# Later start and closer spacing of the modulation sums in a conditioned decoder layer

## The chip, the cores and the metric

The kernel runs on one core of one Trainium2 chip. The metric is the device time of one execution in microseconds (us); lower is better. A core has TensorE (PE, with its weight loads shown as PEld), VectorE (DVE), ScalarE (ACT), GpSimd (POOL) and SyncE (SP), each with its own queue of instructions that it takes in order. Here SP issues all transfers that are named below.

## The reference

One decoder layer on x (1024 tokens by 1024 columns, float32), conditioned by a vector c. Its matrix products are made to float32 accuracy. What matters for the change:

```
mod = silu(c) @ ada_w + ada_b            # 9 blocks of 1024: sh1 sc1 g1 sh2 sc2 g2 sh3 sc3 g3
h = rms_norm(x, norm_g[0]) * (1 + sc1) + sh1
x = x + 0.5 * g1 * ((silu(h @ w1) * (h @ w3)) @ w2)        # first feed-forward
...                                       # mixer with sh2 sc2 g2, second feed-forward with sh3 sc3 g3
```

Blocks 0 and 1 (sh1, sc1) are needed at once. Block 2 (g1) is needed when the first feed-forward's down products are added to x, blocks 3 and 4 for the norm behind that, and blocks 5 to 7 later.

## The kernel before, in words

The program is written in stages: the first feed-forward's up products (units), its down products (rounds), the mixer, and the second feed-forward in the same form. Within a stage the order of instructions is set by a planner (class Plan, L133). Each operation is given to it with an engine, an assumed duration, the tiles it reads and writes, and a rank, which is the time at which it is due. The planner goes through an assumed timeline, takes for each engine the operation that can start first, and among those that can start within 0.2 us the one of lowest rank. So the ranks and the assumed durations fix the order in which each engine gets its work, SP's queue too; the chip then runs each queue in that order.

**The up stage.** The hidden columns are treated in 11 parts of 256 (p = 0 to 10). A fast form of block multiplication with seven products instead of eight is used, numbered i = 1 to 7. A unit (p, i, m) is one product for one of the two weights m; there are 154 units. The first 12 are products 1 and 2 of the first three parts, units 12 to 41 are the other five products of these parts, ten units each, and from unit 42 on a part has fourteen units. A unit's matrix work (Ffn.products, L468) is four groups of three matmuls (mm3, L63, lines 64 to 66), because each operand is split into a rounded high part and a rest. The weights of a unit are split by ScalarE (cast, L57) and VectorE (rest, L60). Some units need sums of weight blocks first (minus, L391 to L395, on VectorE). After a unit its bank is read out by ScalarE (L505, L514) or added by VectorE (L496, L516, L520), and gate and value are multiplied (L524). The hidden blocks and their differences (hidden, L531) go to DRAM. Seven weight buffers (wh and wf) let the weights run ahead of TensorE.

Unit n is due at due1(n) (L906), 2.58 us apart from unit 12 on, and when(n) (L379) is the high part of unit n's weights: an operation with after=when(n) can't start before that cast.

**The modulation's blocks for later parts** are summed on VectorE beside these units (ada_half, L948). Blocks 2 to 7 are cut into halves of 512 columns, so there are twelve halves. For each, eight transfers bring 128 by 512 rows of ada_w (256 KB each, into three buffers named ar), and VectorE multiplies the first by a column of silu(c) (L943) and adds the next seven (L945) in one accumulator (acc, one buffer for all halves). The sum is split in two (ahl, L57 and L60), two matmuls with a matrix of ones add it over the partitions into a bank (psb, L968 and L969), and VectorE turns that row into columns of modc with four multiply-and-sum operations by the identity (ada_columns, L974, line 978) and one to three small ones (L982 to L987). The loop over the halves is at L989 to L993:

```
    halves = [(b, hf) for b in range(2, 8) for hf in range(2)]
    for n, (b, hf) in enumerate(halves):
        u = 24 + 9 * n
        ada_half(f1, b, hf, due1(u), 2.8, f1.when(u - 2), lambda ps, b=b, hf=hf: ada_columns(b, hf, ps), 1.3,
                 w=[("mod", b, hf)])
```

The loads of a half wait for the weights of unit u - 2. Its sums are due from due1(u) on, 2.8 us apart, and its two matmuls 22.4 us after due1(u), 8.7 units later.

**Behind the last half** come eight bias tables for the attention (bias_table, L996). The first waits for the last half, ("mod", 7, 1), and each next one for the store of the one before. Each has one float32 matmul into a bank named psw (L1003) that lies where psb did (tags tr and av). Then come the lambda and gate columns (lam_and_rnn_columns, L1054), a chain of small VectorE operations with two exponentials on ScalarE. The first round of the down stage (Ffn.down, L616) uses the banks tr and av.

Of the kernel before, what the change touches and what calls it, by code (L numbers as in the profile page):

```python
# [44 lines left out]
def layer(tc, I, out):  # L45
# [860 lines left out]
    def due1(n, k=0):  # L906
        if n < 4 * EARLY:
            return 21.0 + 5.0 * (4 * (n // 6) + k) + T_MM3 * (n % 6)
        return 62.0 + 2.58 * (n - 4 * EARLY)
# [38 lines left out]
    def ada_half(f, b, hf, at, pace, when, finish, dur, r=(), w=()):  # L948
        plan = f.plan
        op, the = plan.op, plan.get  # L950
        acc, ps = f"acc{b}_{hf}", f"psb{b}_{hf}"
        new_tile(plan, acc, "acc")
        for k in range(KC):
            a = f"ar{b}_{hf}_{k}"
            new_tile(plan, a, "ar")
            op(SP, lambda a=a, k=k: load(the(a), ada_v[:, k, b * D + hf * TG : b * D + (hf + 1) * TG]), T_LOAD,
               w=[a], rank=at + pace * k - 6, after=when)
            op(DVE, lambda a=a, k=k: ada_sum(the(acc), the(a), k), 0.66, r=[a] + ([acc] if k else []),
               w=[acc, (acc, k)], rank=at + pace * k)
        hl = [f"ahl{b}_{hf}_{s}" for s in range(2)]  # L960
        for s in hl:
            new_tile(plan, s, "k2", None, F32R)
        at += pace * KC
        f.split(lambda: the(hl[0]), lambda: the(hl[1]), lambda: the(acc), [acc], at, hl, hl[1:])
        new_tile(plan, ps, ("tr", "av"))

        def sums():
            T.matmul(the(ps), lhsT=onesr, rhs=the(hl[1]), start=True, stop=False)  # L968
            T.matmul(the(ps), lhsT=onesr, rhs=the(hl[0]), start=False, stop=True)  # L969

        op(PE, sums, 0.43, r=hl, w=[ps], rank=at)
        op(DVE, lambda: finish(the(ps)), dur, r=[ps, *r], w=w, rank=at)

    def ada_columns(b, hf, ps):  # L974
        c0 = b * KC + hf * 4
        for q in range(4):
            junk = fp.tile([P, P], F32, tag="arow", bufs=1, name=f"junk{b}_{hf}_{q}")
            V.tensor_tensor_reduce(
                junk, ps[:, q * P : (q + 1) * P], ident, 1.0, 0.0, ALU.mult, ALU.add, modc[:, c0 + q : c0 + q + 1]
            )  # L980
        mc = modc[:, c0 : c0 + 4]
        V.tensor_tensor(mc, mc, adabc[:, c0 : c0 + 4], ALU.add)  # L982
        if b % 3 == 1:
            o = b // 3 * KC + hf * 4
            V.scalar_tensor_tensor(gmc[:, o : o + 4], mc, 1.0, smc[:, NG0 + o : NG0 + o + 4], ALU.add, ALU.mult)
        if b == 2:
            V.tensor_scalar(mc, mc, 0.5, None, ALU.mult)  # L987

    halves = [(b, hf) for b in range(2, 8) for hf in range(2)]  # L989
    for n, (b, hf) in enumerate(halves):  # L990
        u = 24 + 9 * n
        ada_half(f1, b, hf, due1(u), 2.8, f1.when(u - 2), lambda ps, b=b, hf=hf: ada_columns(b, hf, ps), 1.3,
                 w=[("mod", b, hf)])  # L993

# [744 lines left out]
    for j in range(2):  # L1739
        n = next(nch)  # L1740
# [43 lines left out]
    for dc in range(KC):  # L1784
        n = n0 + dc
# [11 lines left out]
    for dc in range(6):  # L1797
        n = n0 + 8 + dc
# [104 lines left out]
    for hf in range(2):  # L1903
        u, row = 60 + 30 * hf, f"g3r{hf}"
# [132 lines left out]
def build(shapes):  # L2037
    import concourse.bacc as _bacc
    import concourse.tile as _tile

    nc = _bacc.Bacc("TRN2", target_bir_lowering=False, num_devices=1)
    aps = {n: nc.dram_tensor(f"in_{n}", s, F32, kind="ExternalInput").ap() for n, s in shapes.items()}
    out = nc.dram_tensor("out_0", (1, S, D), F32, kind="ExternalOutput").ap()
    with _tile.TileContext(nc, schedule_with_timeline_sim=True) as tc:
        layer(tc, aps, out)
    return nc
# [10 lines left out]
```

## Time and profile before

| | us |
|---|---|
| Runs of the kernel before | 1819.23, 1821.06, 1826.95 |
| Median of the three | 1821.06 |
| The profiled execution's own time | 1820.87 |
| Its span | 1818.3 |
| Mean granted TensorE clock in it | 0.989 of full speed |

The profile is of one execution. Times in it are counted from the span's start. The page gives busy time per engine and 40 slices of the span; the trace answers closer questions, by stretch, by instruction, by wait. "x" before a number is a count. L-numbers are lines of the kernel. Matmuls are pipelined, so the recorded duration of one is longer than the step from one start to the next. In lists in order of time the bracket at the end tells how long the engine was idle before the instruction and what ended that.

### The profile page before, as it was taken

To read this page: it belongs to the slowest core of one execution; us is meant where nothing else is said; L and a number is where in the kernel's file an instruction comes from. 1 tells how busy PE (TensorE), PEld (TensorE's weight loads), DVE (VectorE), ACT (ScalarE), POOL (GpSimd) and SP (SyncE) were. 2 spreads that over 40 slices of the span, in tenths; PEclk is the share of its full clock that TensorE was granted. 3 is DMA by queue.
4 is the path that set the end of the run, shared out by engine and by line. 5 is a ranking of instruction groups with operands and counts; after the bars stand their busy time and mean duration, and the time that the engine had idled before them with its cause. 6 is when DMAs were issued, how large, how long until landed. Compare 5 with 4: busy or idle time off the path is not lost.

```text
span 1818.3 us, 23531 instructions
## 1 busy us (share of the span) xinstructions
PE 1772.9 (98%) x8098; PEld 1456.2 (80%) x8098; DVE 1432.1 (79%) x2739; ACT 854.3 (47%) x1485; POOL 13.0 (1%) x28
## 2 busy tenths in 40 slices
PE   8999999999999999899999989999999999999997
PEld 7877788887788888688888878878888888888886
DVE  3898999887778779788787786598777666579798
ACT  4442443333554334676675854353333333365344
POOL 0000000000000001000000000000000000000000
PEclk8999999999999999999999989999999999999999
DMA  9636666553598663212121435315433333497862
GB/s 272 210 128 229 194 203 207 173 194 118 193 350 272 223 237 121 65 47 76 47 64 58 122 99 180 118 56 174 162 116 128 132 106 109 132 364 266 291 216 93
DMA packets 230136, 297.48 MB, mean 164 GB/s; under 512 B 16733, under 2 KB 125438, under 8 KB 230018
## 3 DMA queue, kind: packets, MB, share of 16 engines
q1 hardware_dynamic: 230018, 296.00, 49.5%
q8 instruction: 63, 1.03, 0.2%
q14 instruction: 55, 0.45, 0.1%
HBM read 228.30 MB, written 63.44 MB: 160 GB/s over the span
## 4 chain that ended last, share of the span: by engine, by line
PE 84%; DVE 9%; DMA 3%; ACT 2%; issue 1%; SPq 1%; DVEq 0%; ACTq 0%
PE f1b L64 6%; PE f2b L64 6%; PE f2b L66 6%; PE f2b L65 6%; PE f1b L66 6%; PE f1b L65 6%; PE pc L64 5%; PE pc L65 5%; PE pc L66 5%; PE f1ps L64 4%; PE f1ps L66 4%; PE f1ps L65 4%; PE f2ps L64 4%; PE f2ps L65 4%; PE f2ps L66 4%; PE psd L879 2%
## 5 line engine op out<-in xcount | busy, mean ns | idle before, releaser
L65 PE MATMUL f1b<-f1B,f1w 128*128 128x512 f32 x616 | 243.0, 394 | 5.7 <-DVE f1w L60 5.6
L64 PE MATMUL f1b<-f1B,f1w 128*128 128x512 f32 x616 | 245.3, 398 | 0.8 <-ACT f1vs L514 0.8
L66 PE MATMUL f1b<-f1B,f1w 128*128 128x512 f32 x616 | 242.4, 394 | 0.0
L64 PE MATMUL f2b<-f2B,f2w 128*128 128x512 f32 x440 | 171.5, 390 | 2.4 <-ACT f2vq L490 1.8
L65 PE MATMUL f2b<-f2B,f2w 128*128 128x512 f32 x440 | 171.5, 390 | 1.2 <-DVE f2w L60 1.2
L66 PE MATMUL f2b<-f2B,f2w 128*128 128x512 f32 x440 | 171.2, 389 | 0.0
L65 PEld LDWEIGHTS f1b<-f1B,f1w 128*128 128x128 f32 x616 | 116.3, 189 | 33.3 <-DVE f1w L60 8.8
L64 PEld LDWEIGHTS f1b<-f1B,f1w 128*128 128x128 f32 x616 | 116.3, 189 | 28.7 <-issue 2.7
L66 PEld LDWEIGHTS f1b<-f1B,f1w 128*128 128x128 f32 x616 | 116.2, 189 | 26.0
L60 DVE TENSOR_TENSOR f2w<-f2r,f2w 128x512 fp32r<-128x512 f32 x124 | 84.5, 688 | 66.2 <-ACT f2w L57 65.2
L64 PE MATMUL pc<-h,wch 128*128 128x512 f32 x320 | 131.1, 410 | 3.1 <-DVE h L1132 1.4
L57 ACT ACTIVATE f2w<-f2r 128x512 fp32r<-128x512 f32 x124 | 76.5, 628 | 110.8 <-issue 42.7
L66 PE MATMUL pc<-h,wch 128*128 128x512 f32 x320 | 125.7, 393 | 0.0
L65 PE MATMUL pc<-h,wcl 128*128 128x512 f32 x320 | 125.6, 393 | 0.0
L64 PE MATMUL f1ps<-f1o,f1d 128*128 128x512 f32 x308 | 121.6, 395 | 0.0
L57 ACT ACTIVATE f1w<-f1r 128x512 fp32r<-128x512 f32 x124 | 75.7, 627 | 97.0 <-DVE f1r L393 31.3
L66 PE MATMUL f1ps<-f1o,f1d 128*128 128x512 f32 x308 | 121.2, 393 | 0.0
L65 PE MATMUL f1ps<-f1o,f1d 128*128 128x512 f32 x308 | 121.0, 393 | 0.0
L64 PE MATMUL f2ps<-f2d,f2o 128*128 128x512 f32 x308 | 119.9, 389 | 0.1
L65 PE MATMUL f2ps<-f2d,f2o 128*128 128x512 f32 x308 | 119.8, 389 | 0.0
L66 PE MATMUL f2ps<-f2d,f2o 128*128 128x512 f32 x308 | 119.8, 389 | 0.0
L64 PEld LDWEIGHTS f2b<-f2B,f2w 128*128 128x128 f32 x440 | 82.6, 188 | 20.6 <-ACT f2vq L490 2.2
(414 smaller groups left out, 3944.3 us busy)
## 6 DMA issues: line engine op xcount, KB each, us to landing
ar<-in_ada_w SPq DMA_DIRECT2D x112, 256.0 KB, 3.3
f2r<-in_ffn_w SPq DMA_DIRECT2D x44, 512.0 KB, 3.7
f1r<-in_ffn_w SPq DMA_DIRECT2D x40, 512.0 KB, 4.0
f1wa<-in_ffn_w SPq DMA_DIRECT2D x38, 512.0 KB, 4.8
f2wa<-in_ffn_w SPq DMA_DIRECT2D x38, 512.0 KB, 5.6
f1b<-f1gt SPq DMA_DIRECT2D x44, 256.0 KB, 4.8
f2b<-f2gt SPq DMA_DIRECT2D x44, 256.0 KB, 5.7
rc<-in_w_in SPq DMA_DIRECT2D x20, 512.0 KB, 3.8
```

The lines of the kernel that those rows point to most:

```text
L57: A.activation(hi, src, AF.Copy)
L60: (eng or V).tensor_tensor(lo, src, hi.bitcast(F32), ALU.subtract)
L64: T.matmul(ps, lhsT=wh, rhs=xl, start=first, stop=False, skip_group_check=more)
L65: T.matmul(ps, lhsT=wl, rhs=xh, start=False, stop=False, skip_group_check=more)
L66: T.matmul(ps, lhsT=wh, rhs=xh, start=False, stop=last, skip_group_check=more)
L879: T.matmul(the(ps)[:, b : b + 1], lhsT=the(aw)[:, n, :], rhs=cact[:, 4 * h + n : 4 * h + n + 1], start=h == 0 and n == 0, stop=h == 1 and ...
```

## The change

The first half is put at unit 40 in place of unit 24, and the distance from one half to the next is eight units in place of nine. So the halves stand at units 40, 48, ... 128, where they stood at 24, 33, ... 123. The pace within a half, 2.8 us from one row to the next, stays as it is. The bias tables and the columns behind them keep their own due times (due1(128) on, and due1(142)).

```
     halves = [(b, hf) for b in range(2, 8) for hf in range(2)]
     for n, (b, hf) in enumerate(halves):
-        u = 24 + 9 * n
+        u = 40 + 8 * n
         ada_half(f1, b, hf, due1(u), 2.8, f1.when(u - 2), lambda ps, b=b, hf=hf: ada_columns(b, hf, ps), 1.3,
                  w=[("mod", b, hf)])
```

## Rows read from the trace of the kernel before

**Rows 1.** The page: busy time per engine, and VectorE's slices in tenths.

```profile
PE 1772.9 (98%) x8098; PEld 1456.2 (80%) x8098; DVE 1432.1 (79%) x2739; ACT 854.3 (47%) x1485; POOL 13.0 (1%) x28
...
DVE  3898999887778779788787786598777666579798
```

**Rows 2.** Stretches: length, busy PE, PEld, DVE, ACT, POOL, then PEclk, DMA share, GB/s.

```profile
160.00:180.00 20.00, 18.15 (x78) 14.14 (x77) 18.86 (x32) 5.75 (x10) 0.00 (x0) 1.00 0.65 213
180.00:200.00 20.00, 18.13 (x79) 14.36 (x78) 18.20 (x37) 8.42 (x15) 0.00 (x0) 1.00 0.61 196
200.00:360.00 160.00, 160.00 (x699) 130.80 (x698) 146.54 (x274) 62.07 (x107) 0.00 (x0) 1.00 0.61 198
1480.00:1560.00 80.00, 80.00 (x354) 66.25 (x353) 51.18 (x77) 29.56 (x50) 0.00 (x0) 1.00 0.30 102
```

**Rows 3.** Chain of waits, 120 to 190 us: shares by line, and its longest piece.

```profile
by line: DMA ar<-in_ada_w 18.0%; DVE f1w L60 14.1%; DVE f1r L393 12.4%; DVE acc L945 9.9%; DMA f1vr<-f1g 8.4%; issue 7.4%; DVE f1vu L520 4.4%; DVE f1vu L393 3.6%; DVE f1vv L496 2.9%; DVE f1vp L520 2.8%; DVE f1s L393 2.6%; DVE f1vp L524 2.0%
...
174.51 6.92 DMA ar<-in_ada_w
```

**Rows 4.** Chain of waits, 205 to 430 us: shares by line.

```profile
by line: PE f1b L66 32.8%; PE f1b L64 32.8%; PE f1b L65 32.7%; PE psb L968 0.9%; PE psb L969 0.9%
```

**Rows 5.** TensorE's instructions in order of time: start, duration, instruction, idle before it.

```profile
163.02 0.39 PE L64 MATMUL f1b<-f1B,f1w 128*128 128x512 f32 x1
165.21 0.50 PE L65 MATMUL f1b<-f1B,f1w 128*128 128x512 f32 x1 [1.80 <-DVE f1w L60]
...
183.94 0.40 PE L66 MATMUL f1b<-f1B,f1w 128*128 128x512 f32 x1
186.20 0.47 PE L968 MATMUL psb<-ahl,onesr 128*128 128x512 f32 x1 [1.87 <-DVE ahl L60]
```

**Rows 6.** VectorE's instructions in order of time, two places.

```profile
128.37 0.48 DVE L943 TENSOR_SCALAR acc<-ar,cact 128x512 f32<-128x512 f32 x1
128.76 0.68 DVE L393 TENSOR_TENSOR f1r<-f1r,f1r 128x512 f32<-128x512 f32 x1
129.37 0.68 DVE L60 TENSOR_TENSOR f1w<-f1r,f1w 128x512 fp32r<-128x512 f32 x1
...
322.85 0.75 DVE L945 SCALAR_TENSOR_TENSOR acc<-ar,cact,acc 128x512 f32<-128x512 f32 x1
323.51 0.68 DVE L60 TENSOR_TENSOR f1w<-f1r,f1w 128x512 fp32r<-128x512 f32 x1
```

**Rows 7.** VectorE by line, 205 to 397 us: busy us, mean ns, idle before.

```profile
L60 DVE TENSOR_TENSOR f1w<-f1r,f1w 128x512 fp32r<-128x512 f32 x62 | 42.4, 687 | 6.0 <-ACT f1w L57 5.5
L945 DVE SCALAR_TENSOR_TENSOR acc<-ar,cact,acc 128x512 f32<-128x512 f32 x56 | 41.8, 746 | 1.9 <-DMA ar<-in_ada_w 1.6
L978 DVE CUSTOM_DVE_ANT_0 junk<-psb,ident 128x128 f32<-128x128 f32 x32 | 9.3, 290 | 1.5 <-PE psb L969 0.4
...
L978 DVE DVE_READ_ACCUMULATOR2_ANT modc<- 128x1 f32 x32 | 2.6, 82 | 0.0
```

**Rows 8.** Row buffers and split sums to 500 us: ns min/median/max, first, last start.

```profile
L943 DVE TENSOR_SCALAR acc<-ar,cact x12: 478/481/487, 128.4 to 394.4; 128x512 f32<-128x512 f32 x12
...
DMA to landing us min/median/max: 2.5/3.3/6.9
...
L60 DVE TENSOR_TENSOR ahl<-acc,ahl x12: 680/684/691, 156.9 to 414.7; 128x512 fp32r<-128x512 f32 x12
```

**Rows 9.** The banks psb, psw and f1b: ns min/median/max, first and last start.

```profile
L969 PE MATMUL psb<-ahl,onesr x12: 390/395/399, 158.0 to 437.1; 128*128 128x512 f32 x12
...
L1003 PE MATMUL psw<-oh,rbb x16: 374/412/479, 439.6 to 468.5; 32*128 32x256 f32 x16
...
L66 PE MATMUL f1b<-f1B,f1w x616: 387/390/629, 28.9 to 504.4; 128*128 128x512 f32 x154
```

**Rows 10.** VectorE's wait at the gate columns; the stretch before the down stage.

```profile
476.77 0.17 DVE L1038 TENSOR_SCALAR lw<-lw 128x4 f32<-128x4 f32 x1 [2.15 <-ACT lw L1065]
...
480.00:500.00 20.00, 20.00 (x90) 16.39 (x89) 16.33 (x38) 12.63 (x23) 0.00 (x0) 1.00 0.70 226
```

More of the change, by code (lines that the diff above doesn't have):

```diff
@@ L990, in layer @@
     for n, (b, hf) in enumerate(halves):
-        u = 24 + 9 * n
+        u = 40 + 8 * n
         ada_half(f1, b, hf, due1(u), 2.8, f1.when(u - 2), lambda ps, b=b, hf=hf: ada_columns(b, hf, ps), 1.3,
```

## The prediction

> **What bounds the kernel now.** I read the page first. TensorE is busy for 98% of the span, so time is lost or won only where TensorE stands still, and in the slices VectorE has its longest full run early, in the first up stage, where the change works [rows 1]. So I cut that stage into stretches [rows 2]; the granted clock is 1.00, the 2.4 GHz level, in all of them. From 160 to 200 us TensorE lacks 1.85 + 1.87 us of 40. From 200 to 360 us it lacks nothing, with VectorE at 146.5 of 160 us, or 92%. The same kind of stage in the second feed-forward, with no modulation sums in this stretch, has VectorE at 51.2 of 80 us, or 64%.
>
> The chain of waits says who is at fault. Between 120 and 190 us almost every piece is VectorE work or a landing of a modulation row, with the largest at 6.92 us [rows 3]. Between 205 and 430 us every named piece is TensorE's own [rows 4]. So the modulation sums hurt early and are free later. TensorE's instructions in order of time show the damage itself [rows 5]. The step from one matmul to the next is about 0.23 us. At 163.02 it is 2.19 us, because weights are late from VectorE, and at 183.94 it is 2.26 us, because TensorE has reached the column sum (psb) of a half whose second operand VectorE has not made.
>
> **Pace and load.** 699 matmuls in 160 us are 0.229 us each [rows 2]. A unit is 12 of them, 2.75 us. Nine units are 24.7 us and eight are 22.0 us.
>
> VectorE's load I take from start to start, because it runs these operations closer together than their recorded durations: 0.39 us for the first product of a half, 0.61 us for a tensor_tensor, 0.66 us for a multiply-add [rows 6]. The four diagonal sums I take with their accumulator reads at 0.29 + 0.08 us each [rows 7]. A half costs 0.39 + 7 x 0.66 + 0.61 + 4 x 0.37 + 0.3 = 7.4 us, where 0.3 us is an estimate for its one to three column operations, from the 0.17 us of such small ones [rows 10]. By the code units 12 to 41, the first three parts, need 35 tensor_tensors per ten units: 10 weight rests, 8 weight sums, 4 for the value pairs, 6 additions from the banks, 3 products and 4 differences. That is 35 x 0.61 = 21.4 of 27.5 us, 78%. Later parts need 36 per fourteen units, 22.0 of 38.5 us, 57%.
>
> **The change part by part.** Nothing is added or taken away: twelve halves, 96 row loads, 12 x 7.4 us of VectorE and 24 TensorE column sums remain. They move.
>
> *Out of units 24 to 39.* A half every nine units is 7.4 of 24.7 us, 30%. On the 78% of the first three parts that is 108%: VectorE cannot keep up, and the lead that weights should have over TensorE is gone at 163 and 184 us. Without it, 78% leaves room. The two gaps go: 2.19 - 0.23 and 2.26 - 0.23, 1.96 + 2.03 = 4.0 us. Smaller ones I leave out. As bounds I keep 0 (other work makes the same gaps) and 6.0, one more gap of that size in the sums' first 40 us, which the rows don't cover. What would be late next is a weight load or a reload of a hidden block; neither made TensorE wait in these gaps.
>
> *Into units 40 to 137, denser.* A half every eight units is 7.4 of 22.0 us, 34%; on 57% that is 91%, where nine units gave 87%. The recorded busy share of 92% would rise by 4 points to about 96%. Cover remains, since spare VectorE time is what hides this work; without it each of the 97 units would lose its excess. I take 0, with bounds 0 and the 5 us worked out next.
>
> VectorE's recorded durations, 0.69 us for the tensor_tensor and 0.75 us for the multiply-add [rows 7], would fill it: 36 x 0.69 + 14/8 x 8.2 = 39.2 of 38.5 us, where 8.2 us is the half by durations. That is 0.7 us lost in each 14 units, 5 us over 97 units if weights start with no lead. The Trainium skill (VectorE: DVE Perf Modes, The DRAIN you can't avoid) states that the next operation starts only when the pipe has emptied, and its errata section gives (N+151)/0.96, 691 ns at 512 elements, for a float32 tensor_tensor. The trace agrees with that duration and not with the spacing, 0.61 us: that page of the Trainium skill itself lets an operation that is not held start earlier. By the rule the sum would be about 1821.9 us.
>
> *The loads.* The row loads move on SP's queue by sixteen units at the front and five at the end, past weight loads and stores of the hidden blocks. The worst landing, 6.9 us against a median of 3.3 [rows 8], lies in the early stretch. Three row buffers stay. A load that waits on SP for one of them holds the weight loads and stores queued behind it; from 200 to 360 us the same mix passes with no loss on TensorE [rows 2]. I take 0; the bounds are 0 and 2.0 us, one gap like that at 183.94.
>
> *The end.* The last half is summed by unit 136.7 instead of 131.7, so 5 x 2.75 = 13.8 us later. TensorE's last column sum, at 437.1 [rows 9], comes at about 451. The eight bias tables wait for it. They now take from 439.6 to 468.5 [rows 9] and would end near 482; the stage's matmuls end at 504.4 [rows 9], less the gain. The tables' banks (tr and av) are wanted by the first down round then, and are free some 18 us before. The lambda and gate columns follow the tables: VectorE waits 2.15 us for an exponential there [rows 10], and would do so near 490. VectorE has 16.3 busy of 20 us at 480 to 500 [rows 10], so 3.7 us of spare stand beside that wait. I take 0; the bounds are 0 and 2.2 us, that wait passed on to TensorE in full.
>
> **Sum.** 1820.87 - 4.0 = 1816.9 us, against the profiled execution's own time, 0.2 us from the median of the runs shown, 1821.06.
>
> **The rivals.**
> *The gaps only move.* The first halves then run into weight loads of 2 MB per part at units 40 to 50, and TensorE waits there for a late row as at 183.94. For it: that gap was a landing of 6.92 us. Against it: the later halves run in the kind of units into which all are now put, and between 205 and 430 us no wait of TensorE is in the chain [rows 4]. All 4.0 us come back: 1820.9.
> *VectorE is the bound* by its durations: 1821.9, as worked out. Against it: the spacing, and that nine units would already come to 98% that way, with no wait on TensorE seen.
> *The column sum waits half after half* (slower than before). One accumulator serves all halves, so each must finish inside its spacing. The last half before takes from its first product at 394.4 to its rest at 414.7, 20.3 us [rows 8]; now it has 22.0 where it had 24.7. If a half takes over 22.0 us, the lead of 22 us that the last one has over its column sum (437.1 - 414.7) is eaten up, and TensorE stands in order at psb. If six of twelve halves then pay 2.03 us, that is 12.2 us: 1820.9 - 4.0 + 12.2 = 1829.1. For it: the first half took 28.5 us (128.4 to 156.9). Against it: that was under 108% load.
> *More is won.* With the sums out of the way, VectorE's lead at unit 40 would also have to close other gaps, over 9 us in all: below 1811.9. Against it: past 200 us rows 2 show none left to close.
> *The change does less than it says*, because halves are started by weights and run ahead of their due times anyway: the gate stands two units before the unit, so it must move. I give this nothing of its own.
>
> **How the numbers follow.** The forecast gets 0.68, gaps that move 0.15, VectorE as the bound 0.04, the waiting column sum 0.09, more 0.04. At the low end the range takes in the gain of 6.0 us, 1814.9, less 3.9 us, half of the 7.7 us between the fastest and the slowest of the runs shown: 1811.0. At the high end it takes in the rivals at 1820.9 and 1821.9 and one stall of 2.0 us on top: 1823.9. A difference of 0.5%, 9.1 us, is about what a measurement of this kernel can tell from no change. The forecast is 0.2%, so it lies within. Faster by more is the last rival, 0.04. Slower by more needs the column sum to wait in more than half of the halves, or something not seen: 0.07. The rest, 0.89, is the same.
>
> **What would show it.** Right: no gap over 1 us between 116 and 500 us on TensorE; the first product of a half about 40 us later, near 168; VectorE near 96% in the later stretch; the chain from 120 to 190 us on TensorE; last column sum near 447 (451 less the gain); tables ended before the down stage. Wrong: waits of psb for the rest of a half after 200 us, weights late from VectorE in units 40 to 137, TensorE waiting at 480 to 520 us, or a gap in the first three parts that stays without the sums.

## The result and the profile after

| | before | after the change |
|---|---|---|
| Median of 20 runs each, us | 1822.93 | 1814.32 |
| Lowest and highest, us | 1816.34, 1830.79 | 1808.80, 1820.88 |
| Profiled execution, its span, us | 1820.87, 1818.3 | 1820.0, 1818.2 |

The ratio is 0.995, with an interval from 0.9939 to 0.9961: 9.1 us less, between 7.1 and 11.1. Of two later sets of runs of the same change one gave 0.9958 (0.9939 to 0.9977) and one 0.9963 (0.9948 to 0.9977), 7.7 and 6.7 us. So the change gains 7 to 9 us where 4.0 were forecast. The profiled execution of the change is one of its slowest, at a mean granted clock of 0.988, where the execution of 1808.8 us had 0.993; its span against that of before hides the gain, and stages have to be compared, in more than one profile.

The page of the changed kernel, busy time and VectorE's slices, to be held against [rows 1]:

```profile
PE 1776.1 (98%) x8098; PEld 1460.2 (80%) x8098; DVE 1432.6 (79%) x2739; ACT 855.4 (47%) x1485; POOL 13.0 (1%) x28
...
DVE  3798999998778779789687787598777666579798
```

The same instructions have run, and the run of full slices of VectorE is two slices longer. The stretches of the changed kernel, with the columns of [rows 2]:

```profile
160.00:180.00 20.00, 20.00 (x88) 16.34 (x88) 18.40 (x31) 6.37 (x11) 0.00 (x0) 1.00 0.76 252
180.00:200.00 20.00, 20.00 (x88) 16.33 (x87) 18.73 (x29) 9.95 (x17) 0.00 (x0) 1.00 0.65 205
200.00:360.00 160.00, 160.00 (x696) 130.31 (x695) 147.45 (x281) 61.23 (x104) 0.00 (x0) 1.00 0.63 200
...
480.00:500.00 20.00, 20.00 (x87) 15.91 (x86) 16.61 (x56) 12.72 (x22) 0.00 (x0) 1.00 0.62 192
```

From 160 to 200 us TensorE now lacks nothing, where it lacked 1.85 + 1.87 us. The sums' own rows to 520 us, in the tile views of ar and psb (ns min/median/max, first and last start), answer to [rows 8, 9]:

```profile
L943 DVE TENSOR_SCALAR acc<-ar,cact x12: 478/486/491, 168.2 to 411.9; 128x512 f32<-128x512 f32 x12
...
DMA to landing us min/median/max: 2.6/3.2/5.6
```

```profile
L969 PE MATMUL psb<-ahl,onesr x12: 392/394/399, 202.1 to 450.6; 128*128 128x512 f32 x12
```

The first product starts at 168.2 us, the last column sum at 450.6, and the worst landing of a row is 5.6 us. Up to here the profile is what was forecast, but for VectorE's share from 200 to 360 us: 147.45 of 160 us are 92%, as before, where about 96% was forecast. Where more of the gain may lie, TensorE's waits between 720 and 1000 us show, in the norm behind the first feed-forward and most of the mixer. Columns: what waited, for what, us in total, times, longest. The view of waits of the kernel before:

```profile
PE s L1388 <- ACT p L1406: 5.7, 3, 4.1
PE pc L64 <- DVE h L1132: 1.4, 1, 1.4
PE pc L64 <- DVE h L393: 0.9, 1, 0.9
```

The changed kernel:

```profile
PE s L1388 <- DMA kl<-kl: 2.3, 1, 2.3
PE s L1388 <- ACT p L1406: 1.7, 1, 1.7
PE pc L64 <- DVE h L1132: 0.8, 1, 0.8
PE pc L65 <- DVE wcl L1254: 0.6, 1, 0.6
PE pg L64 <- ACT y L1530: 0.3, 1, 0.3
PE pc L64 <- DVE h L393: 0.3, 1, 0.3
```

No line there was edited, yet other waits stand in it: the two for the normed h (L1132, L393) are 1.2 us shorter, the one of 4.1 us for the first exponentials of the attention (p, L1406) is 1.7 us, and a wait of 2.3 us for a transfer (kl, the rest of the attention's keys) is new. So these stages were planned anew. TensorE's instructions in order of time at that exponential, before:

```profile
751.16 0.33 PE L1388 MATMUL s<-kl,q 128*128 128x128 f32 x1 [4.13 <-ACT p L1406]
...
752.58 0.63 PE L65 MATMUL pc<-h,wcl 128*128 128x512 f32 x1
753.00 0.63 PE L66 MATMUL pc<-h,wch 128*128 128x512 f32 x1
753.43 0.42 PE L1388 MATMUL s<-kl,q 128*128 128x256 f32 x1
```

and after:

```profile
750.99 0.33 PE L1388 MATMUL s<-kl,q 128*128 128x128 f32 x1 [1.73 <-ACT p L1406]
...
752.01 0.40 PE L65 MATMUL pc<-h,wcl 128*128 128x512 f32 x1
752.25 0.40 PE L66 MATMUL pc<-h,wch 128*128 128x512 f32 x1
```

Behind the idle 4.13 us the matmuls step 0.42 us from one to the next (752.58 to 753.00); behind 1.73 us they step 0.24. The granted clock of the stretches says the same. Before (length, PE, PEld, DVE, ACT, POOL, PEclk, DMA share, GB/s):

```profile
720.00:760.00 40.00, 33.50 (x146) 26.75 (x145) 30.40 (x67) 24.59 (x45) 3.41 (x3) 0.96 0.48 130
880.00:920.00 40.00, 39.32 (x197) 32.44 (x196) 27.88 (x77) 26.37 (x49) 0.62 (x2) 1.00 0.22 59
```

After:

```profile
720.00:760.00 40.00, 36.64 (x167) 28.83 (x166) 31.53 (x74) 26.46 (x48) 3.50 (x3) 1.00 0.45 123
880.00:920.00 40.00, 37.66 (x173) 31.20 (x172) 26.56 (x75) 23.60 (x44) 0.62 (x2) 0.91 0.22 60
```

TensorE fits 167 matmuls into the first stretch instead of 146 and stays at 2.4 GHz, and gives some of it back behind the wait for kl near 900 us, where the granted clock is 0.91 and 173 matmuls pass instead of 197.

**Stage lengths.** Two stages differ between the kernels, and I read their lengths from every profile. The up stage is counted from TensorE's last matmul ahead of its wait for L514 (0.82 us, near 90 us) to the start of the last f1b matmul: 89.57 to 504.4 before, 414.8 us; 91.47 to 504.3 after, 412.8. The norm and mixer are counted from the last f1ps matmul to the last pc<-h matmul: 719.6 to 1046.8 before, 327.2 us; 719.4 to 1045.3 after, 325.9. The down stage between them is 215.1 or 215.2 us in all profiles but two (220.1 in e4, 214.7 in e10). One profile can be off by some 3 us in each, so the profiles of all runs are taken together below.

### The profile page after: what moved, and what is told of

It reads as the page before. It is cut to its first block, busy times and chain, and to the rows that moved or that the text cites. A ratio compares the mean times of both kernels' runs of the same rounds, so it can differ in the third digit from the quotient of the medians.

```text
span 1818.2 us, 23570 instructions
## 1 busy us (share of the span) xinstructions
PE 1776.1 (98%) x8098; PEld 1460.2 (80%) x8098; DVE 1432.6 (79%) x2739; ACT 855.4 (47%) x1485; POOL 13.0 (1%) x28
## 4 chain that ended last, share of the span: by engine, by line
PE 86%; DVE 8%; DMA 2%; ACT 2%; issue 1%; SPq 0%; ACTq 0%; DVEq 0%
PE f1b L64 7%; PE f1b L66 7%; PE f1b L65 7%; PE f2b L64 6%; PE f2b L65 6%; PE f2b L66 6%; PE pc L64 5%; PE pc L65 5%; PE pc L66 5%; PE f1ps L66 4%; PE f1ps L64 4%; PE f1ps L65 4%; PE f2ps L64 4%; PE f2ps L66 4%; PE f2ps L65 4%; PE psd L879 2%
## 5 line engine op out<-in xcount | busy, mean ns | idle before, releaser
L57 ACT ACTIVATE f1w<-f1r 128x512 fp32r<-128x512 f32 x124 | 76.8, 628 | 102.1 <-PE f1b L66 38.5
```

What stands on the lines that cost most here:

```text
L57: A.activation(hi, src, AF.Copy)
```

## The experiments

Two theories stood for the gaps in the up stage. By the first (the load, letter A where letters are used) VectorE has too much to do in the first three parts. By the second (the landings, letter B) late rows of ada_w hold the sums, and with them what is queued behind. A third question came with the result: what the replanned norm and mixer bring. The measured columns give the ratio to runs of the kernel before on the same chip, and the difference as (ratio - 1) x 1822 us.

| run | up, us | norm and mixer, us | both, against 742.7 | ratio (95%) | measured, us |
|---|---|---|---|---|---|
| before, first profile | 414.8 | 327.2 | -0.7 | | |
| e1 before again | 415.4 | 328.0 | +0.7 | 0.9995 (0.9981 to 1.0009) | -0.9 |
| the change, first | 412.8 | 325.9 | -4.0 | 0.9950 (0.9939 to 0.9961) | -9.1 |
| e2 the change again | 411.2 | 322.7 | -8.8 | 0.9958 (0.9939 to 0.9977) | -7.7 |
| e12 the change, third | 410.6 | 324.9 | -7.2 | 0.9963 (0.9948 to 0.9977) | -6.7 |
| e3 spacing alone | 418.3 | 327.1 | +2.7 | 1.0015 (0.9999 to 1.0032) | +2.7 |
| e4 start alone | 407.9 | 323.9 | -10.9 | 0.9951 (0.9932 to 0.9971) | -8.9 |
| e7 short sums | 411.7 | 327.1 | -3.9 | 0.9984 (0.9970 to 0.9999) | -2.9 |
| e8 one load | 413.3 | 328.4 | -1.0 | 0.9975 (0.9960 to 0.9991) | -4.6 |
| e5 mixer order of the change | 415.9 | 328.1 | +1.3 | 0.9998 (0.9983 to 1.0012) | -0.4 |
| e11 the same again | 415.0 | 325.2 | -2.5 | 1.0006 (0.9989 to 1.0023) | +1.1 |
| e6 mixer order of before | 410.7 | 326.5 | -5.5 | 0.9982 (0.9965 to 0.9999) | -3.3 |
| e9 start 32, spacing 8 | 411.0 | 327.1 | -4.6 | 0.9970 (0.9954 to 0.9986) | -5.5 |
| e10 start 40, spacing 7 | 409.1 | 324.5 | -9.1 | 0.9951 (0.9933 to 0.9968) | -8.9 |

742.7 is the mean of the two profiles of the kernel before, (742.0 + 743.4) / 2.

**The two kernels again.** Nothing is edited in e1 and e2.

> The kernel before, a second time, for another profile of it. Both theories expect a ratio of 1.000 within 0.002. Theory A (the early sums overload VectorE) expects gaps of TensorE between 150 and 200 us again, together 4 to 9 us, at late weights or at the column sums. Theory B (the gaps come from row loads that happened to land late in one execution) expects their sum and places to differ, and possibly none.

> The changed kernel, a second time, for another profile of it. Both theories expect a ratio near 0.995. Theory A expects at most 2 to 3 us of gaps between 116 and 500 us, so that nearly all of the gain is read in that stage. Theory C (a part of the gain lies outside the up stage, in the start or in the stages behind) expects the up stage to be shorter by only 2 to 4 us and the rest of the 9 us to stand elsewhere.

The kernel before is equal to itself within 0.2%, and the change holds. In e2, TensorE's waits in the up stage (80 to 520 us, the view of waits) come to 4.3 us, where the kernel before has 8.5.

**Which of the two numbers pays.** e3 keeps the start and takes the spacing, e4 the other way round:

```
-        u = 24 + 9 * n
+        u = 24 + 8 * n      # e3
+        u = 40 + 9 * n      # e4
```

> Spacing alone: u = 24 + 8 n, the start left at unit 24. Theory A (load in the first three parts decides) expects VectorE's load there to rise from 108% to 112%, gaps of 5 to 12 us between 140 and 200 us, and a ratio of 1.000 to 1.003. A theory by which the denser spacing or the earlier end is what pays expects 0.995 to 0.998.

> Start alone: u = 40 + 9 n, the spacing left at nine units. The last half is due at unit 147.7, so the eight bias tables run into the first down round, whose banks they share. Theory A expects the early gaps to go as in the change, and so a ratio of 0.995 if the tables find room at the round's bounds, or up to 10 us more if TensorE waits for them. A theory by which the spacing pays expects 0.998 to 1.000 with no wait at the tables.

The later start pays: the ratio of e4 lies clear of 1. Denser sums from unit 24 on do not, and they may cost: the interval of e3 is 0.9999 to 1.0032. TensorE's waits of e3 between 80 and 520 us:

```profile
PE f1b L65 <- DVE f1w L60: 7.3, 7, 3.2
PE f1b L64 <- ACT f1vs L514: 0.8, 1, 0.8
PE f1b L64 <- ACT f1w L57: 0.6, 1, 0.6
PE psb L968 <- DVE ahl L60: 0.4, 2, 0.2
```

Weights are late from VectorE seven times, where the kernel before has three such waits (5.6 us). The column sum waits for only 0.4 us in all, where it waited 2.1 us, although VectorE has more to do. e4 has the shortest up stage, but its tables run into the down stage, which is 220.1 us long instead of 215.2. So of its -10.9 us 4.9 are given back, -6.0 in sum. In TensorE's order of time the matmul of a table waits there for its row:

```profile
499.72 0.69 PE L1003 MATMUL psw<-oh,rbb 32*128 32x256 f32 x2 [1.31 <-DVE rbb L1001]
```

The time of e4 is that of the change, within the intervals: with the later start the closer spacing makes no difference that was measured; it puts the tables ahead of the down stage.

**Load or landings.** e7 leaves all but 32 of the 512 columns out of seven of the eight products of a half; e8 loads only one row per half and uses it eight times, so the other seven rows are left out.

```
-            V.scalar_tensor_tensor(acc, r, c, acc, ALU.mult, ALU.add)
+            V.scalar_tensor_tensor(acc[:, 0:32], r[:, 0:32], c, acc[:, 0:32], ALU.mult, ALU.add)      # e7
```

```
-            op(SP, lambda a=a, k=k: load(the(a), ada_v[:, k, b * D + hf * TG : b * D + (hf + 1) * TG]), T_LOAD,
+            op(SP, lambda a=a, k=k: k or load(the(a), ada_v[:, k, b * D + hf * TG : b * D + (hf + 1) * TG]), T_LOAD,      # e8
...
-            op(DVE, lambda a=a, k=k: ada_sum(the(acc), the(a), k), 0.66, r=[a] + ([acc] if k else []),
+            op(DVE, lambda k=k: ada_sum(the(acc), the(f"ar{b}_{hf}_0"), k), 0.66, r=[a] + ([acc] if k else []),
```

> The kernel before, with the seven multiply-adds of each half shortened from 512 to 32 columns (the rest of the modulation row is left out), all loads and the order of instructions kept. Theory A (VectorE's load): no gap over 1 us between 140 and 200 us, the up stage 4 us shorter, the mixer as before, ratio 0.998. Theory B (late landings of row loads): the gap at the column sum near 184 us stays, only the one at the weights goes.

> The kernel before, with one row load per half instead of eight; all eight sums read that one row (the other seven rows of the modulation weights are left out), VectorE's work and its order kept. Theory A: the gaps between 140 and 200 us stay at 3 us or more, ratio 0.999 to 1.000. Theory B: they go, ratio 0.998.

The gap at the column sum, 184 us before [rows 5], goes in both runs; in the other profiles of this up stage it is 1.9, 1.2, 1.0 and 1.7 us (before, e1, e5, e11). So it needs both, the full sums and all their loads. Neither theory expected this: A had it go with the sums alone, B with the loads alone. The gap at 163 us stays in both. In e8 (TensorE in order of time):

```profile
161.68 0.39 PE L64 MATMUL f1b<-f1B,f1w 128*128 128x512 f32 x1
163.85 0.50 PE L65 MATMUL f1b<-f1B,f1w 128*128 128x512 f32 x1 [1.79 <-DVE f1w L60]
```

In e7:

```profile
163.90 0.39 PE L64 MATMUL f1b<-f1B,f1w 128*128 128x512 f32 x1
166.05 0.50 PE L65 MATMUL f1b<-f1B,f1w 128*128 128x512 f32 x1 [1.76 <-DVE f1w L60]
```

VectorE in the same kernel, ahead of that weight:

```profile
159.30 0.29 DVE L978 CUSTOM_DVE_ANT_0 junk<-psb,ident 128x128 f32<-128x128 f32 x1 [0.73 <-PE psb L969]
...
162.11 0.24 DVE L945 SCALAR_TENSOR_TENSOR acc<-ar,cact,acc 128x32 f32<-128x32 f32 x1
...
164.10 0.69 DVE L496 TENSOR_TENSOR f1vv<-f1vp,f1b 128x512 f32<-128x512 f32 x1 [0.54 <-PE f1b L66]
164.70 0.68 DVE L393 TENSOR_TENSOR f1vv<-f1vv,f1vp 128x512 f32<-128x512 f32 x1
165.31 0.69 DVE L60 TENSOR_TENSOR f1w<-f1r,f1w 128x512 fp32r<-128x512 f32 x1
```

The multiply-add takes 0.24 us here and VectorE is not full: it waits 0.73 us for the column sum and 0.54 us for a bank of TensorE's. The rest that TensorE needs is queued behind both and ends at 166.0: the readout of the bank (L496) starts at 164.10, when TensorE is through with it, and the readout, one difference (L393) and the rest then take 1.9 us, while TensorE stands for 1.76. So at 163 us the lateness lies in the order of VectorE's queue and not in the duration of the sums. The gap, of 1.76 to 1.97 us, stands in all seven profiles with the start at unit 24 and in none of the seven with a later start. That the work of the column sums in between is what puts the rest so far back is argued; no run reorders it alone. The time of e8 (-4.6 us) is not found in its two stages (-1.0); its interval goes from -1.6 to -7.3 us.

**The norm and the mixer.** When the plan of the first feed-forward and the norm is done, the times at which it lets each engine end go to the plan of the mixer. e5 gives the kernel before the end times of the change at this point (after `plan.run()`, L1168), and e6 gives the change those of before:

```
     plan.run()
+    t_pe = plan.now[PE]
+    plan.now = {e: t_pe + v for e, v in {'PE': 0.0, 'Act': 8.531, 'DVE': 9.351, 'Pool': -10.082, 'SP': -10.202}.items()}      # e5
+    plan.now = {e: t_pe + v for e, v in {'PE': 0.0, 'Act': 9.214, 'DVE': 10.034, 'Pool': -9.721, 'SP': -10.634}.items()}      # e6
+    plan.port = {e: plan.now[e] for e in (DVE, POOL)}
...
     was = plan
```

The end times of h2 and qf00 are set in the same way. e11 is e5 once more.

> The kernel before, with only the mixer planned from the engine times that the changed kernel's up and down stages leave relative to TensorE (ScalarE and VectorE 0.68 us earlier). The up stage is untouched. Theory M (a second part of the gain is the mixer's order of instructions, which the planner makes anew from these times): the 4.1 us wait of TensorE for the first exponential and the half-clock matmuls behind it go, the mixer is 3 to 4 us shorter, ratio 0.998, and the early gaps stay. Theory U (all of the gain is in the up stage, the mixer differs by chance between executions): ratio 1.000, mixer 327 to 328 us from the last down matmul to the last projection.

> The changed kernel, with only the mixer planned from the engine times that the kernel before leaves relative to TensorE. Theory M: the early gaps stay away, but the 4.1 us wait at the first exponential comes back and the mixer is again 327 to 328 us; ratio 0.997 to 0.998. Theory U: ratio 0.995 to 0.996, as the change.

> The kernel before with the mixer planned from the changed kernel's times, a second time. Theory M': its time multiplied by its granted clock is 3 to 4 us under that of the kernel before, and the ratio lies anywhere from 0.998 to 1.000 as half-clock stretches take it back. If the mixer's order is worth nothing, both are unchanged.

TensorE's waits from 720 to 1000 us in e5 (lines behind the edit are four further down, in e6 too):

```profile
PE s L1392 <- DMA kl<-kl: 2.2, 1, 2.2
PE s L1392 <- ACT p L1410: 1.7, 1, 1.7
PE pc L64 <- DVE h L1132: 1.4, 1, 1.4
PE pc L64 <- DVE h L393: 0.9, 1, 0.9
...
```

and in e6:

```profile
PE s L1392 <- ACT p L1410: 5.8, 3, 4.2
PE pc L64 <- DVE h L1132: 0.8, 1, 0.8
PE pc L64 <- DVE h L393: 0.5, 2, 0.3
PE pc L64 <- ACT y L1534: 0.4, 1, 0.4
```

The end times differ by 0.7 us for ScalarE and VectorE and 0.4 us for GpSimd and SyncE, and those of some blocks of h2 by up to 2.5 us. This is enough to turn the mixer's order into the other one, in both directions, while the waits of the norm stay with the up stage's plan. The mixer's order by itself brings nothing that the runs' times show: e5 and e11 stand at -0.4 and +1.1 us, with intervals from -3.1 to +2.2 and from -2.0 to +4.2, where theory M had forecast 0.998. Taken out of the change it may cost: e6 has -3.3 us, where the change has -6.7 to -9.1, but its interval, down to -6.4, overlaps two of the change's three. The stage lengths do show a difference. Seven profiles have the old order (before, e1, e3, e6, e7, e8, e9), and their norm and mixer take 326.5 to 328.4 us, 327.3 on average; seven have the new one (the change's three, e4, e5, e10, e11), with 322.7 to 328.1, 325.0 on average: 2.3 us less.

The clock in this stage does not explain why so little of that arrives. The old order loses some of it at 720 to 760 us in all its seven profiles (0.91 in e1 and e8, 0.96 in the others) and none at 880 to 920. The new order mostly has 1.00 in the first stretch (0.97 in e5, 0.96 in e10), and at 880 to 920 us 0.91 in the first profile of the change and in e5, 0.96 in e4, e11 and e12, 1.00 in e2 and e10. Added up over both stretches of 40 us, either order lacks 15 us of full clock in seven profiles.

**Other places for the sums.** e9 starts eight units earlier than the change, e10 packs the halves closer, and e12 is the change a third time, beside them:

```
-        u = 24 + 9 * n
+        u = 32 + 8 * n      # e9
+        u = 40 + 7 * n      # e10
+        u = 40 + 8 * n      # e12
```

> Start at unit 32 in place of 40, spacing eight: u = 32 + 8 n. The planner then gives the up stage the change's length but the mixer the order of the kernel before. Theory M' (the gain is the up stage with the handoff, 5 us, plus the mixer's order, some 3 us of full-clock time that half-clock stretches can take back): ratio 0.997 to 0.998, the 4.1 us wait at the first exponential back. Theory U' (all of it comes with the sums leaving the first parts): 0.995.

> Denser: u = 40 + 7 n. VectorE's load behind unit 40 is 57% + 38% = 95% from start to start, and 107% by recorded durations. If recorded durations counted, TensorE would lose 2.6 us in each fourteen units, 16 us over the 86 units, ratio 1.004. If each half has to wait for the one before (19.3 us of spacing against 20.3 us needed), the column sums would wait up to 1 us each. If the spacing of starts counts, no gap over 1 us between 160 and 450 us, ratio 0.995.

> The changed kernel a third time, beside the other three on one chip. Theory M': time multiplied by granted clock 7 to 9 us under the kernel before, ratio 0.995 to 0.996, the up stage 3 to 5 us shorter and the mixer's head with no 4 us wait.

e9 is a kernel with an up stage as short as that of the change (411.0 us) and the norm and mixer of before: its waits from 720 to 1000 us are the three of before, 5.7, 1.4 and 0.9 us. It gains 5.5 us (2.6 to 8.4), which is a second measure, beside e6, of what the up stage brings by itself. e10 from 200 to 360 us, in the columns of the stretches:

```profile
200.00:360.00 160.00, 160.00 (x699) 130.88 (x698) 150.21 (x296) 62.31 (x106) 0.00 (x0) 1.00 0.65 206
```

By recorded durations a half every seven units is 8.2 of 19.25 us, 43%, and with 36 x 0.69 of 38.5 us, 65%, VectorE would be at 107% and lose 7% of 84 units, 16 us. It is busy for 94%, TensorE stands nowhere, and 699 matmuls pass as before. So operations count by the step from one start to the next, by which the load is 57% + 38% = 95%. The Trainium skill (VectorE: DVE Perf Modes, The DRAIN you can't avoid) has the next operation start only when the pipe is empty, and adds that one that is not held starts earlier; the traces agree with the second, with 0.61 us from start to start for 0.68 recorded [rows 6]. e10 beats the kernel before by 8.9 us and stands level with the change (6.7 to 9.1).

## Why the prediction was right or wrong

**Out of units 24 to 39: right in size.** The forecast was -4.0 us. Four profiles with the change's up stage (the change, e2, e12 and e6) have 411.3 us on average, four with that of before (before, e1, e5 and e11) 415.3: -4.0 us. Both named gaps are gone, and no psb wait is left. The chain of waits from 120 to 190 us is TensorE's own work for 59%, not all of it. The reason was half of it. Load has a part in the gap at 184 us, which goes with shorter sums, but it goes with fewer loads too and nearly goes in e3, where the load is higher; the extra late weights of e3 fit the load. The gap at 163 us stays when the sums are shortened to 32 columns, so it does not need a load of 108%. It goes when all the work of the sums goes elsewhere.

**Into later units, denser: right in its cost, off in VectorE's share.** The share was to rise by 4 points, from 92% to about 96%. From 200 to 360 us, where the 92% was read, it rises by 0.6 points, from 146.54 to 147.45 of 160 us, and 281 operations of VectorE fall into this stretch where 274 did. From 200 to 430 us its busy time goes from 205.9 to 212.8 of 230 us, 3.0 points, to 92.5%, near the 91% that the sum of starts gave. TensorE stands nowhere, though it passes 999 matmuls there where it passed 1003, 0.9 us of its pace; what slows it wasn't tried. That VectorE is the bound by its durations (+5 us) falls with e10.

**The loads: right.** SP's first row load starts at 160.6 us, the worst landing is 5.6 us, and no gap of TensorE's in the up stage names a row. Two gaps of the first profile, 0.7 and 1.0 us at 128.7 and 149.0 us, lie ahead of the first row load and are not the sums'; the second, 1.04 us, is just over the 1 us that was named as a sign, and in e2 and e12 neither is there.

**The end: right.** Column sum 450.6 for 451; the last table matmul at 480.5 and its copy at 483.1 for 482; TensorE is full from 480 to 500 us. The last half takes 18.8 us from its first product (411.9) to its rest (430.7), below the 22.0 it has, so the rival of the waiting column sum had no ground. How near the end is shows in e4, whose last half stands eleven units later: its down stage is 4.9 us longer.

**What failed** is the frame of the part on the change, that only sums, loads and tables move, and with it the sentence against the rival that more is won: "past 200 us rows 2 show none left to close". That looked for gaps in the up stage alone, while the planner hands its end times to what follows. The terms that were missing: the waits for h, 1.4 + 0.9 to 0.8 + 0.3 us, and the mixer's order. Together the norm and mixer are 327.6 us before (327.2, 328.0) and 324.5 after (325.9, 322.7, 324.9): -3.1 us. By these five profiles the sum is -4.0 - 3.1 = -7.1 us, inside two of the three measured intervals and at the edge of the first (-7.1 to -11.1). By all fourteen, with 2.3 us for the norm and mixer, it is -6.3. The mixer's share is read from profiles alone; e5 and e11 do not confirm it. Gain and place of the first term were right, the forecast total was about half of what came. That the time stands near the forecast is in part luck: the sum started from 1820.87 us, and the median of the 20 runs of the kernel before is 1822.93. The range held the time, 1814.32, not by its bound of 6.0 us on that term (1814.9) but by the spread of the runs taken off below it.

The chances suffered from the same gap: 0.04 stood for faster by over 0.5%, and the measured ratio lies on that line.

**What stays open.** By the measured times the parts add up to less than the whole: the up stage and norm with the old mixer order give -3.3 us (e6), the new mixer order -0.4 and +1.1 (e5, e11), the change -6.7 to -9.1. The intervals just allow it. e11 and e12 also had a forecast for each run's time multiplied by its mean granted clock, and there the parts do add up. On average over the runs, against the kernel before in the same set, e6 and e9 have 5.5 and 5.7 us less, e5 and e11 3.8 and 1.5, e2 and e12 7.2 and 7.5. (e12 was forecast at 7 to 9, e11 at 3 to 4, which it misses.) In e5 and e11 the mean granted clock of the runs is 0.0016 and 0.0009 below that of the kernel before, and this takes back what the order gains. The two stretches above do not show where it is lost, and such means vary by as much; whether it is chance or belongs to the order is open.

## What to carry to other kernels

Where a planner orders the work, a change of due times in one stage is a change of every stage that is planned from its end times: compare the waits of later stages too. Where work fills idle time of an engine, add up that engine's load by starts, not by recorded durations (94% against 107% in e10). A gap behind a late operation should be tested with the load taken away, since it may be one of order. With runs that spread by 12 us, one pair of profiles can hide a gain of 8; stage lengths from several of them showed it.

## What the hardware showed that was not expected

The same program's mean granted clock differs from execution to execution: 0.993 at 1808.8 us, 0.984 at 1820.88 us, both the change. Behind the same idle time TensorE falls to 1.2 GHz in some executions only. After a wait of 3.2 us for a weight, the longest of the up stage in every profile, which ends at 104 to 111 us, the clock of the stretch from 80 to 120 us is 1.00 in seven profiles (before, the first of the change, e4, e8, e10, e11, e12) and 0.96 in the other seven. VectorE, busy for 94% of 160 us by recorded times in e10, did not hold TensorE up once in that stretch.
